# Weight sums, PSUM evictions and residual sums of a hybrid layer's channel sub-layer, arranged another way

## The chip, the cores and the metric

The kernel runs on one core of a Trainium2 chip. The metric is the device time of one execution in microseconds (us); lower is better. The kernel before takes 2641.09 us (median of three runs, 2638.81 to 2647.72).

A core has a matrix engine (TensorE, PE in the profile; PEld is its weight load), a vector engine (VectorE, DVE), a scalar engine (ScalarE, ACT), a general engine (GpSimd, POOL) and SyncE (SP), which here issues transfers (DMAs). Each engine takes its instructions strictly in the order in which the built program lists them; they wait for each other by semaphores. SBUF is the on-chip memory that all engines work in, PSUM the small memory into which the matrix engine accumulates, DRAM the large memory where inputs, outputs and scratch tensors lie.

## The reference

The reference is one decoder layer on a sequence of 512 positions and 2048 features, in 32-bit floats. A mixing sub-layer (a gated linear recurrence and an RWKV-7 head group) comes first; the change touches nothing of it. The channel sub-layer and the final norm follow, cut here to what matters:

```python
h = modulate(rms_norm(x, norm_ffn_g[l]), sh_f, sc_f)
gate, up = jnp.split(h @ w_gu[l], 2, axis=-1)
x = x + g_f[:, None, :] * ((jax.nn.silu(gate) * up) @ w_down[l])
...
return rms_norm(x, final_norm_g)
```

w_gu is 2048 x 11264 and w_down 5632 x 2048. The row g_f gates the result of the second product, feature by feature, before it is added to the residual x.

## The kernel before

**Products.** Both products are done in a Strassen-Winograd form: a pair of 2 x 2 blocks is multiplied with seven block products in place of eight. A block product's weight operand is a block of weights or a sum of blocks. Called b11, b12, b21 and b22, the four blocks go in as: product 1 takes b11, product 6 takes s = b11 + b12 + b22, product 5 takes b11 + b12, product 4 takes b21 + s, product 7 takes b12 + b22, product 2 takes b21 and product 3 takes b22. Every operand is split into a high and a low part (`whi` by a cast on ACT, L105; `wlo` by a subtraction on DVE, L106), and three matmuls, high by high, low by high and high by low, give nearly full 32-bit accuracy.

**Stages and loops.** The up projection (weights `w_gu`) has 11 column blocks m of 8 k-tiles a half. The down projection (weights `w_down`) is done in three chunks of 8, 7 and 7 k-tiles a half, each with two column blocks m. One column block runs through `half` twice: the first half makes the products 1, 6, 5, 4, the second 7, 2, 3. A half has four steps k0 of two k-tiles (or one, at the end of 7). A step loads its blocks into tiles `wraw` (tag "raw", 8 buffers of 512 KB, which the staging of the left operands shares), adds, splits, and issues twelve matmuls of 128 x 512 for each product of two k-tiles. The split tiles `whi` and `wlo` have four buffers each.

**Sums of weights.** In the first half three additions on DVE make the operands (L1269, L1270 and L1276), in the second one (L1285).

**PSUM.** Products 1 and 7 use the banks of tag "mm", 6 and 2 of "gr", 5 and 3 of "ch", two banks each, one for each half t of the rows; product 4 uses "st" and "y". When the last step's matmuls of a product are issued, `finish(p, t)` takes its PSUM out and combines it with what is kept: a copy on ACT for product 1 (L1237), and additions or subtractions on DVE for the others (L1240 for product 6, L1243 for 5, L1246 for 4, L1249 and L1250 for 7, L1254 for 2, L1257 for 3). The next column block's product 1 needs the "mm" banks that L1249 and L1250 read. The results live in tiles `ev_a`, `ev_b`, `ev_v` and `ev_w`, one buffer for each t.

**Order.** A list scheduler sets the order on every engine when the program is built, from the dependencies, its own cost estimates and priorities; code inside `tc.high_priority()` goes ahead of what is not. The sums and the splits are in such blocks; `finish` is not. At run time the order is fixed.

**Results of the down projection.** `down_end` has `put(x, t, e)` for each of the 16 result tiles (four row blocks t, four column groups e) of a chunk. Chunk 0 stores them to scratch tensors `yd` in DRAM. Chunk 1 fetches `yd` back, adds it on POOL (L1091) and stores it again. Chunk 2 fetches and adds once more, fetches the gate row (`gf`, broadcast to all partitions), multiplies on DVE (L1096), fetches the residual `x1d`, adds it on DVE (L1097), and squares on ACT for the norm (L1099). Results of e = 0 and 2 go to `xd` in DRAM and come back as `xend`; those of e = 1 and 3 stay in SBUF. All these transfers are issued by SP (L1085, L1093, L1101, L1163), in one queue with the weight loads (L1211). Behind the last chunk stand the loads of the norm's weights `fg` and `xend`, the root and reciprocal of the norm (L1166 to L1168), and 16 scalings on DVE (L1172), each with its store of the output.

## Time and profile before

| what | value |
|---|---|
| median of three runs | 2641.09 us (2638.81 to 2647.72) |
| the profiled execution's own time | 2636.42 us |
| its span, first to last instruction | 2634.3 us |
| mean granted clock of TensorE | 0.949 |
| busy over the span | PE 2345.7 us, DVE 2096.4, ACT 1117.4, POOL 260.1 |
| up projection | about 1076 to 2038 us |
| down projection | about 2038 to 2574 us |
| last matmul to the end | 2574 to 2634.3 us |

The profile is of one execution. "x52" in a row is a count; a number in square brackets behind an instruction is how long its engine sat idle ahead of it and what released it. SPq is SP's issuing queue: a wait there holds every transfer that stands behind it. The granted clock is a share of full speed. The DMA share is the mean busy share of the core's 16 DMA engines.

### The profile page before, as it was taken

What the parts mean: (1) busy time and instruction counts of PE and PEld (TensorE: products, weight loads), DVE (VectorE), ACT (ScalarE), POOL (GpSimd) and SP (SyncE); (2) the same over time, 40 slices, a digit from 0 to 9 for tenths busy, and PEclk for the clock granted to TensorE, in tenths of its full rate; (3) what the DMA queues carried; (4) which work ended last, traced back from release to release, by engine and by line L of the source; (5) the groups of instructions that cost most, each with busy time, mean ns of one, the idle gap of its engine ahead of it and who ended that gap; (6) DMA issues with size and microseconds to landing.
All of it is one profiled execution on the core that took longest, in us unless ns stands there. A gap on an engine that the chain in (4) does not pass through costs nothing. (4 is left out here: it accounts for less than half of the span.)

```text
span 2634.3 us, 32326 instructions
## 1 busy us (share of the span) xinstructions
PE 2345.7 (89%) x10992; PEld 1856.6 (70%) x10992; DVE 2096.4 (80%) x3730; ACT 1117.4 (42%) x1625; POOL 260.1 (10%) x207
## 2 busy tenths in 40 slices
PE   6999999999998989779899999999999998987980
PEld 4667777777777867557778777787777776765760
DVE  7879898999887657878788777778779988788764
ACT  3356455454464333534334434444444444333331
POOL 0000111111001000130000000000003112234101
PEclk9999999999999999789999999999999999998985
DMA  8864534454524267546667656666557767676664
GB/s 310 302 210 120 158 113 144 135 153 142 155 73 137 74 210 253 184 160 213 227 225 246 188 177 197 193 200 192 182 180 236 233 226 250 205 236 237 201 222 148
DMA packets 265977, 503.47 MB, mean 191 GB/s; under 512 B 23442, under 2 KB 48402, under 8 KB 261586
## 3 DMA queue, kind: packets, MB, share of 16 engines
q1 hardware_dynamic: 265812, 501.41, 59.0%
q8 instruction: 86, 1.41, 0.2%
q14 instruction: 79, 0.65, 0.1%
HBM read 466.84 MB, written 34.10 MB: 190 GB/s over the span
## 5 line engine op out<-in xcount | busy, mean ns | idle before, releaser
L105 ACT CAST whi<-wraw 128x1024 fp32r<-128x1024 f32 (+1 forms) x707 | 625.9, 901 | 908.2 <-DVE wraw L1270 250.8
L106 DVE TENSOR_TENSOR wlo<-wraw,whi 128x1024 fp32r<-128x1024 f32 (+1 forms) x707 | 742.0, 1067 | 245.3 <-ACT whi L105 240.9
L1227 PE MATMUL ps_mm<-whi,comb 128*128 128x512 f32 x528 | 216.7, 411 | 53.7 <-DVE ev_b L1250 34.4
L1227 PE MATMUL ps_gr<-whi,comb 128*128 128x512 f32 x528 | 217.7, 412 | 36.1 <-ACT whi L105 35.3
L124 PE MATMUL ps_mm<-hhi,whi 128*128 128x512 f32 x556 | 235.7, 426 | 8.4 <-ACT hhi L255 6.7
L199 DVE SCALAR_TENSOR_TENSOR adaq<-adaq,cbq 128x512 f32<-128x512 f32 x256 | 174.4, 688 | 73.4 <-DMA adaq<-in_w_ada 59.5
L125 PE MATMUL ps_mm<-hlo,whi 128*128 128x512 f32 x556 | 225.6, 406 | 1.1 <-DVE hlo L256 1.0
L126 PE MATMUL ps_mm<-hhi,wlo 128*128 128x512 f32 x556 | 225.9, 406 | 0.0
L1229 PE MATMUL ps_gr<-wlo,comb 128*128 128x512 f32 x528 | 214.4, 408 | 9.8 <-DVE wlo L106 9.8
L1229 PE MATMUL ps_mm<-wlo,comb 128*128 128x512 f32 x528 | 214.6, 407 | 9.5 <-DVE wlo L106 9.5
L1227 PE MATMUL ps_ch<-whi,comb 128*128 128x512 f32 x528 | 210.7, 399 | 5.1 <-DVE x L996 2.5
L1228 PE MATMUL ps_gr<-whi,comb 128*128 128x512 f32 x528 | 214.3, 406 | 0.0
L1228 PE MATMUL ps_mm<-whi,comb 128*128 128x512 f32 x528 | 214.2, 406 | 0.0
L1229 PE MATMUL ps_ch<-wlo,comb 128*128 128x512 f32 x528 | 209.4, 397 | 1.9 <-DVE wlo L106 1.9
L1228 PE MATMUL ps_ch<-whi,comb 128*128 128x512 f32 x528 | 209.9, 398 | 0.0
L1227 PEld LDWEIGHTS ps_mm<-whi,comb 128*128 128x128 f32 x528 | 103.6, 196 | 83.4 <-DVE ev_b L1250 38.4
L1227 PEld LDWEIGHTS ps_gr<-whi,comb 128*128 128x128 f32 x528 | 104.2, 197 | 65.1 <-ACT whi L105 40.3
L1229 PEld LDWEIGHTS ps_gr<-wlo,comb 128*128 128x128 f32 x528 | 103.3, 196 | 39.4 <-DVE wlo L106 15.5
L124 PEld LDWEIGHTS ps_mm<-hhi,whi 128*128 128x128 f32 x556 | 106.3, 192 | 33.0 <-ACT hhi L255 9.0
L1229 PEld LDWEIGHTS ps_mm<-wlo,comb 128*128 128x128 f32 x528 | 103.5, 196 | 35.1 <-DVE wlo L106 12.9
L125 PEld LDWEIGHTS ps_mm<-hlo,whi 128*128 128x128 f32 x556 | 106.4, 191 | 25.7 <-DVE hlo L256 5.2
L1227 PEld LDWEIGHTS ps_ch<-whi,comb 128*128 128x128 f32 x528 | 101.0, 191 | 31.1 <-DVE ev_v L1257 4.2
(386 smaller groups left out, 4620.3 us busy)
## 6 DMA issues: line engine op xcount, KB each, us to landing
wraw<-in_w_gu SPq DMA_DIRECT2D x308, 512.0 KB, 4.3
wraw<-in_w_down SPq DMA_DIRECT2D x140, 512.0 KB, 4.6
adaq<-in_w_ada SPq DMA_DIRECT2D x256, 256.0 KB, 3.5
wraw<-in_w_in SPq DMA_DIRECT2D x160, 256.0 KB, 3.1
ada<-in_w_ada SPq DMA_DIRECT2D x32, 1024.0 KB, 7.3
stage<-s SPq DMA_DIRECT2D x28, 512.0 KB, 5.0
s<-flip SPq DMA_DIRECT2D x44, 256.0 KB, 3.0
wraw<-in_w_out SPq DMA_DIRECT2D x17, 512.0 KB, 6.1
```

What stands on the lines that cost most here:

```text
L105: nc.scalar.copy(out=hi, in_=src)
L106: nc.vector.tensor_tensor(out=lo, in0=src, in1=hi.bitcast(F32), op=ALU.subtract)
L124: mm(ps, lhsT=w[0], rhs=x[0], start=start, stop=False)
L125: mm(ps, lhsT=w[0], rhs=x[1], start=False, stop=False)
L126: self.pe = mm(ps, lhsT=w[1], rhs=x[0], start=False, stop=stop).ins
L199: nc.vector.scalar_tensor_tensor(out=t, in0=t, scalar=1.0, in1=cb, op0=ALU.mult, op1=ALU.mult, accum_out=part[:, m, h:h + 1])
L1227: mm(ps[p][t], lhsT=ah, rhs=hi[:, z], start=k == 0, stop=False)
L1228: mm(ps[p][t], lhsT=al, rhs=hi[:, z], start=False, stop=False)
L1229: mm(ps[p][t], lhsT=ah, rhs=lo[:, z], start=False, stop=k == n - 1)
```

## The change

Three things are changed, all of them in the channel sub-layer.

First, two of the four weight sums move from DVE to transfers. A new helper `add` issues, on POOL's queue, a transfer from DRAM that adds what it reads to what lies in the tile. In the first half b11 is loaded twice, and b12 is added to the second copy (t1 = b11 + b12); b12 itself is no longer loaded. In the second half b22 is added to the loaded b12 (t3). The sums s and b21 + s stay on DVE.

Second, `finish` is put into a high-priority block.

Third, a result of the down projection is multiplied by its gate in every chunk, on DVE, and in the first two chunks a transfer on POOL's queue adds it to the residual `x1d` in DRAM. The `yd` tensors and the additions on POOL leave. The gate rows are fetched at the start of the second half of each m. For the odd column groups the residual is loaded ahead into tiles `xin`, and `fg`, `xin` and `xend` are loaded ahead of the last second half (chunk 2, m = 1) instead of after it.

```diff
--- before.py
+++ after.py
@@ -982,7 +982,6 @@
                     t = sd[c, e, q] = self.dram.tile([P, w, S], F32, name=f"s{c}{e}{q}")
                     for z in range(w):
                         where[base + e * n + 4 * q + z] = t[:, z]
-        yd = [[self.dram.tile([P, S], F32, name=f"yd{t}{e}") for e in range(4)] for t in range(4)]
 
 
         quads = self.x1q
@@ -1080,22 +1079,20 @@
         ss = self.fq.tile([P, 4, 4], F32, tag="ss", name="ss", bufs=1)
         kept = {}
 
-        def fetch(src, tag):
-            t = fq.tile([P, S], F32, tag=tag[0], name="fetch", bufs=tag[1])
+        def fetch(src, tag, bufs):
+            t = fq.tile([P, S], F32, tag=tag, name="fetch", bufs=bufs)
             nc.sync.dma_start(out=t, in_=src)
             return t
 
         def down_end(c):
             def put(x, t, e):
-                if c:
-                    pool_tt(out=x, in0=x, in1=fetch(yd[t][e], ("ft", 2)), op=ALU.add)
+                tt(out=x, in0=x, in1=self.gate[e], op=ALU.mult)
                 if c < 2:
-                    nc.sync.dma_start(out=yd[t][e], in_=x)
+                    nc.gpsimd.dma_start(out=self.x1d[t][e], in_=x, accum_op=ALU.add)
                     return
-                g = fetch(self.gf[:, e * S:(e + 1) * S].to_broadcast([P, S]), ("ad", 2))
-                tt(out=x, in0=x, in1=g, op=ALU.mult)
-                tt(out=x, in0=x, in1=fetch(self.x1d[t][e], ("ft", 2)), op=ALU.add)
-                junk = fq.tile([P, S], F32, tag="ad", name="junk", bufs=2)
+                x1 = self.xin[t, e] if e % 2 else fetch(self.x1d[t][e], "ft", 2)
+                tt(out=x, in0=x, in1=x1, op=ALU.add)
+                junk = fq.tile([P, S], F32, tag="cb", name="junk", bufs=1)
                 nc.scalar.activation(out=junk, in_=x, func=AF.Square, accum_out=ss[:, t, e:e + 1])
                 if e % 2 == 0:
                     nc.sync.dma_start(out=self.xd[t][e // 2], in_=x)
@@ -1135,6 +1132,24 @@
                 for second in (False, True):
                     if not z and not m and second:
                         h_second()
+                    if z and second:
+                        self.gate = {e: fetch(self.gf[:, e * S:(e + 1) * S].to_broadcast([P, S]), "ad", 2)
+                                     for e in (m, m + 2)}
+                    if z == 3 and m and second:
+                        self.xin = {}
+                        fg = self.big.tile([P, 4, S], F32, tag="h", name="fg")
+                        for e in (1, 3):
+                            v = self.cp.tile([P, 4, S], F32, tag="c", name="xin")
+                            for t in (2, 3, 0, 1):
+                                nc.sync.dma_start(out=v[:, t], in_=self.x1d[t][e])
+                                self.xin[t, e] = v[:, t]
+                        nc.sync.dma_start(out=fg, in_=i["final_g"].to_broadcast([P, D]).rearrange(
+                            "p (e n) -> p e n", n=S))
+                        for e in (0, 2):
+                            v = self.cp.tile([P, 4, S], F32, tag="c", name="xend")
+                            for t in range(4):
+                                nc.sync.dma_start(out=v[:, t], in_=self.xd[t][e // 2])
+                                kept[t, e] = v[:, t]
                     steps = self.half(st, m, second)
                     for j in range(4):
                         if not z and not m and not second:
@@ -1155,13 +1170,6 @@
                     nc.sync.dma_start(out=self.gf.rearrange("o (k p) -> p (o k)", p=P), in_=self.mod[:, 80:96])
 
 
-        fg = self.big.tile([P, 4, S], F32, tag="h", name="fg")
-        nc.sync.dma_start(out=fg, in_=i["final_g"].to_broadcast([P, D]).rearrange("p (e n) -> p e n", n=S))
-        for e in (0, 2):
-            v = self.big.tile([P, 4, S], F32, tag="h", name="xend")
-            for t in range(4):
-                nc.sync.dma_start(out=v[:, t], in_=self.xd[t][e // 2])
-                kept[t, e] = v[:, t]
         r = self.small.tile([P, 4], F32, tag="rstd", name="rstd", bufs=1)
         nc.vector.tensor_reduce(out=r, in_=ss, op=ALU.add, axis=AX.X)
         nc.scalar.activation(out=r, in_=r, func=AF.Sqrt, scale=1.0 / D, bias=self.eps[:, 0:1])
@@ -1210,6 +1218,10 @@
             t = t.rearrange("p (k n) -> p k n", n=S)[:, :w]
             nc.sync.dma_start(out=t, in_=stage["src"](m, k0, w, which).rearrange("k p n -> p k n"))
             return t
+
+        def add(t, which, k0, w):
+            nc.gpsimd.dma_start(out=t, in_=stage["src"](m, k0, w, which).rearrange("k p n -> p k n"),
+                                accum_op=ALU.add)
 
         def product(p, b, k0, w):
             with tc.high_priority():
@@ -1228,7 +1240,8 @@
                     mm(ps[p][t], lhsT=al, rhs=hi[:, z], start=False, stop=False)
                     mm(ps[p][t], lhsT=ah, rhs=lo[:, z], start=False, stop=k == n - 1)
                 if k0 + w == n:
-                    finish(p, t)
+                    with tc.high_priority():
+                        finish(p, t)
 
         def finish(p, t):
             keep, q = self.keep, ps[p][t]
@@ -1263,27 +1276,26 @@
             if not second and k0 == 0:
                 flips, self.pending = self.pending, None
             if not second:
-                b11, b12, b22, b21 = (load(z, k0, w) for z in (0, 2, 3, 1))
+                b11, t1, b22, b21 = (load(z, k0, w) for z in (0, 0, 3, 1))
+                add(t1, 2, k0, w)
                 product(1, b11, k0, w)
                 with tc.high_priority():
-                    tt(out=b11, in0=b11, in1=b12, op=ALU.add)
-                    tt(out=b12, in0=b11, in1=b22, op=ALU.add)
-                product(6, b12, k0, w)
+                    tt(out=b22, in0=t1, in1=b22, op=ALU.add)
+                product(6, b22, k0, w)
                 if flips:
                     flips(0)
                     flips(1)
                 with tc.high_priority():
-                    tt(out=b21, in0=b21, in1=b12, op=ALU.add)
-                product(5, b11, k0, w)
+                    tt(out=b21, in0=b21, in1=b22, op=ALU.add)
+                product(5, t1, k0, w)
                 if flips:
                     flips(2)
                     flips(3)
                 product(4, b21, k0, w)
             else:
-                b12, b22, b21 = (load(z, k0, w) for z in (2, 3, 1))
-                with tc.high_priority():
-                    tt(out=b12, in0=b12, in1=b22, op=ALU.add)
-                product(7, b12, k0, w)
+                t3, b22, b21 = (load(z, k0, w) for z in (2, 3, 1))
+                add(t3, 3, k0, w)
+                product(7, t3, k0, w)
                 product(2, b21, k0, w)
                 product(3, b22, k0, w)
             yield
```

The priorities move instructions. The first place is DVE where one column block of the up projection ends and the next begins (`wraw` are weights, `wlo` split parts; the number is the buffer's). Before:

```order
L106 TENSOR_TENSOR wlo_15519<-wraw_15510,whi_15518 128x1024
L1249 TENSOR_TENSOR ev_w_15241<-ps_mm_15265,ev_w_15241 128x512
L1269 TENSOR_TENSOR wraw_15510<-wraw_15510,wraw_15512 128x1024
L1250 TENSOR_TENSOR ev_b_15451<-ev_v_15221,ps_mm_15265 128x512
L1270 TENSOR_TENSOR wraw_15512<-wraw_15510,wraw_15514 128x1024
L1064 TENSOR_TENSOR ev_w_15241<-ev_w_15241,ev_b_15451 128x512
L1276 TENSOR_TENSOR wraw_15516<-wraw_15516,wraw_15512 128x1024
L106 TENSOR_TENSOR wlo_15539<-wraw_15512,whi_15538 128x1024
L106 TENSOR_TENSOR wlo_15574<-wraw_15510,whi_15573 128x1024
L106 TENSOR_TENSOR wlo_15608<-wraw_15516,whi_15607 128x1024
L1249 TENSOR_TENSOR ev_w_15249<-ps_mm_15266,ev_w_15249 128x512
L1250 TENSOR_TENSOR ev_b_15462<-ev_v_15229,ps_mm_15266 128x512
```

Here `finish` of t = 0 (L1249, L1250) stands between the sums of the next block's first step, its t = 1 stands behind three splits. With the change, at such a place:

```order
L106 TENSOR_TENSOR wlo_14844<-wraw_14794,whi_14843 128x1024
L106 TENSOR_TENSOR wlo_14878<-wraw_14868,whi_14877 128x1024
L1283 TENSOR_TENSOR wraw_14992<-wraw_14990,wraw_14992 128x1024
L1262 TENSOR_TENSOR ev_w_14599<-ps_mm_14623,ev_w_14599 128x512
L1262 TENSOR_TENSOR ev_w_14607<-ps_mm_14624,ev_w_14607 128x512
L1289 TENSOR_TENSOR wraw_14994<-wraw_14994,wraw_14992 128x1024
L1267 TENSOR_TENSOR ev_a_14537<-ps_gr_14641,ev_a_14537 128x512
L1267 TENSOR_TENSOR ev_a_14545<-ps_gr_14642,ev_a_14545 128x512
L106 TENSOR_TENSOR wlo_14897<-wraw_14872,whi_14896 128x1024
L1263 TENSOR_TENSOR ev_b_14809<-ev_v_14579,ps_mm_14623 128x512
L1263 TENSOR_TENSOR ev_b_14820<-ev_v_14587,ps_mm_14624 128x512
L1270 TENSOR_TENSOR ev_v_14579<-ps_ch_14659,ev_v_14579 128x512
```

Both rows of L1262, the first reading of "mm", and both of L1263, which gives it free, now stand together ahead of the splits of products 5 and 4, and ahead of all of them stands L1283 on wraw_14992. That is the sum s of the next block's second step, which reads wraw_14990, the tile into which the plain load and the accumulating transfer of that step went. Behind it stand L1289 (b21 + s) and L1267 (product 2 out of PSUM). The same order stands at the middle of each of the three chunks of the down projection (m = 0 to m = 1).

The second place is SP's queue in the last chunk. Before, in its last column block (`wraw` are weight loads):

```order
L1085 DMA fetch_20379<-gf_17416 128x512
L1085 DMA fetch_20408<-yd00_10428 128x512
L1211 DMA wraw_20699<-in_w_down 128x512
L1211 DMA wraw_20760<-in_w_down 128x2x512
L1085 DMA fetch_20414<-x1d00_9427 128x512
L1211 DMA wraw_20762<-in_w_down 128x2x512
L1211 DMA wraw_20764<-in_w_down 128x2x512
L1101 DMA xd31_10452<-ev_b_20361 128x512
L1085 DMA fetch_20411<-gf_17416 128x512
L1085 DMA fetch_20420<-yd02_10430 128x512
L1211 DMA wraw_20821<-in_w_down 128x2x512
L1211 DMA wraw_20823<-in_w_down 128x2x512
```

and with the change, at the start of the last second half:

```order
L1219 DMA wraw_20736<-in_w_down 128x2x512
L1098 DMA xd11_10432<-ev_v_20114 128x512
L1151 DMA xend_20724<-xd00_10429 128x512
L1151 DMA xend_20724<-xd10_10431 128x512
L1151 DMA xend_20724<-xd20_10433 128x512
L1151 DMA xend_20724<-xd30_10435 128x512
L1151 DMA xend_20729<-xd01_10430 128x512
L1151 DMA xend_20729<-xd11_10432 128x512
L1151 DMA xend_20729<-xd21_10434 128x512
L1151 DMA xend_20729<-xd31_10436 128x512
L1219 DMA wraw_20738<-in_w_down 128x2x512
L1219 DMA wraw_20795<-in_w_down 128x2x512
```

The fetches of `yd` are gone from between the weight loads, and the eight `xend` loads stand there, behind one load of weights (wraw_20736) and ahead of the next (wraw_20738).

## Prediction

> **What bounds the kernel now.** First the windows by stage (columns: window, length, busy time and count of PE, PEld, DVE, ACT and POOL, granted clock, DMA share, GB/s), since a share over the whole span mixes stages:
>
> ```profile
> 1180.00:2000.00 820.00, 784.39 (x3413) 633.06 (x3411) 643.41 (x701) 339.48 (x376) 8.31 (x3) 0.98 0.64 204
> 2000.00:2574.00 574.00, 505.72 (x2032) 393.88 (x2030) 462.59 (x433) 220.59 (x254) 124.20 (x52) 0.93 0.68 224
> 2574.00:2634.30 60.30, 0.01 (x1) 0.00 (x0) 27.62 (x39) 7.37 (x18) 9.68 (x7) 0.52 0.47 160
> ```
>
> Matmuls of one product start 0.227 us apart in the timeline below (1625.48 to 1625.71, for one), so 3413 of them need 775 us of the first window's 820 and 2032 need 461 of the second's 574. The matrix engine sets the pace; 45 us are lost in the up projection, 113 in the down projection, and all 60.3 behind the last matmul. DVE, at 643 of 820 us, is not the bound, so DVE work removed is worth only what the lost time gives back. Then the waits of PE, first of the up projection's window (1180 to 2000), then of the down projection's (2038 to 2574):
>
> ```profile
> PE ps_mm L1227 <- DVE ev_b L1250: 31.5, 11, 5.8
> ```
>
> ```profile
> PE ps_gr L1227 <- ACT whi L105: 15.8, 7, 8.6
> PE ps_gr L1229 <- DVE wlo L106: 9.8, 9, 2.5
> PE ps_mm L1229 <- DVE wlo L106: 8.7, 5, 4.2
> PE ps_mm L1227 <- ACT whi L105: 7.5, 3, 4.0
> PE ps_st L1227 <- ACT whi L105: 6.8, 2, 5.0
> PE ps_mm L1227 <- ACT ev_a L1237: 6.1, 1, 6.1
> PE ps_mm L1227 <- DVE ev_b L1250: 2.9, 2, 2.1
> ```
>
> The up projection loses its time where a column block ends: product 1 of the next waits until L1250 has freed its bank. The timeline of PE and DVE at one such place, and of PE at one of the worst:
>
> ```profile
> 1625.48 0.39 PE L1228 MATMUL ps_mm<-whi,comb 128*128 128x512 f32 x1
> 1625.71 0.39 PE L1229 MATMUL ps_mm<-wlo,comb 128*128 128x512 f32 x1
> ...
> 1626.39 0.39 PE L1229 MATMUL ps_mm<-wlo,comb 128*128 128x512 f32 x1
> 1629.14 0.50 PE L1227 MATMUL ps_mm<-whi,comb 128*128 128x512 f32 x1 [2.36 <-DVE ev_b L1250]
> ```
>
> ```profile
> 1618.05 1.23 DVE L106 TENSOR_TENSOR wlo<-wraw,whi 128x1024 fp32r<-128x1024 f32 x1 [1.53 <-ACT whi L105]
> ...
> 1628.40 0.68 DVE L1250 TENSOR_TENSOR ev_b<-ev_v,ps_mm 128x512 f32<-128x512 f32 x1
> 1629.00 0.68 DVE L1254 TENSOR_TENSOR ev_a<-ps_gr,ev_a 128x512 f32<-128x512 f32 x1
> ```
>
> ```profile
> 1372.74 0.79 PE L1227 MATMUL ps_mm<-whi,comb 128*128 128x512 f32 x1 [5.73 <-DVE ev_b L1250]
> 1373.34 0.63 PE L1228 MATMUL ps_mm<-whi,comb 128*128 128x512 f32 x1
> ...
> 1378.46 0.46 PE L1228 MATMUL ps_gr<-whi,comb 128*128 128x512 f32 x1
> ```
>
> **The tail: -34.5 us.** Behind the last matmul the results pass one by one through a chain: fetch of `yd`, POOL addition, fetch of the gate, multiplication, fetch of the residual, addition.
>
> ```profile
> 2573.62 0.40 PE L1229 MATMUL ps_ch<-wlo,comb 128*128 128x512 f32 x1
> ...
> 2616.22 0.69 DVE L1096 TENSOR_TENSOR ev_v<-ev_v,fetch 128x512 f32<-128x512 f32 x1 [3.23 <-DMA fetch<-gf]
> 2616.95 0.69 DVE L1097 TENSOR_TENSOR ev_v<-ev_v,fetch 128x512 f32<-128x512 f32 x1
> ```
>
> From 2574.0 to 2617.6 are 43.6 us. With the change gates and odd residuals lie in SBUF, and on DVE stand one eviction and thirteen multiplications and additions, which start 0.65 us apart when nothing holds them up (0.60 between the two rows at 1628 above, 0.73 from L1096 to L1097 at the end): 14 x 0.65 = 9.1. The norm, the 16 scalings and the stores stay. Gain 34.5; if the last accumulations into the residual were late it would be less, but the m = 1 results of chunk 1 are summed a whole chunk ahead.
>
> **The column ends of the up projection: +29 us.** The cast and the DVE sums, by the groups of instructions:
>
> ```profile
> L105 ACT CAST whi<-wraw 128x1024 fp32r<-128x1024 f32 (+1 forms) x707 | 625.9, 901 | 908.2 <-DVE wraw L1270 250.8 <-PE ps_mm L125 114.2 <-PE ps_ch L1228 97.2
> ...
> L1269 DVE TENSOR_TENSOR wraw<-wraw 128x1024 f32<-128x1024 f32 x68 | 87.5, 1286 | 0.6
> L1270 DVE TENSOR_TENSOR wraw<-wraw 128x1024 f32<-128x1024 f32 x68 | 86.0, 1264 | 4.6 <-DMA wraw<-in_w_down 3.7
> L1285 DVE TENSOR_TENSOR wraw<-wraw 128x1024 f32<-128x1024 f32 x68 | 84.5, 1243 | 29.0 <-DMA wraw<-in_w_gu 18.8 <-DMA wraw<-in_w_down 9.3 <-DVE wlo L106 0.5
> ```
>
> L1269 and L1285 leave, 172 us, mostly off PE's path. What counts is the row L1283 for the next block's second step, which the new order puts ahead of both L1262. It can run only when a plain load and then an accumulating transfer have landed. Call the two together X. I follow the chain backwards from the end of the block's last product (time 0; a product is 12 x 0.227 = 2.72 us). Only four split buffers exist, so product 3 of the third step, six products from the end, is split when the product four ahead of it is through, at -10 x 2.72 = -27.2, and its cast (0.9 over all forms, 1.0 taken for a full tile) and subtraction (1.2, the row at 1618) end at -25.0. That frees the raw buffer for t1 of the next block's first step. Then follow X, L1283 (1.25, as L1270), a split (1.2), L1289 (1.25) and product 7's split (1.2), 4.9 together, which frees the buffer for t1 of the second step; then X again, L1283 (1.25), two L1262 (1.3), L1289 (1.25), two L1267 (1.3), product 6's split (1.2) and L1263 (0.65), 6.95 together. PE starts at -25.0 + 2X + 11.85, a stall of 2X - 13.15.
>
> X is shown by no row: no transfer in the trace accumulates, and none of these is issued by POOL. Landing times of plain loads, from the weight loads' line and from the list of transfers:
>
> ```profile
> DMA to landing us min/median/max: 2.5/4.3/14.7
> ```
>
> ```profile
> wraw<-in_w_down SPq DMA_DIRECT2D x28, 256.0 KB, 3.6
> ...
> ada<-in_w_ada SPq DMA_DIRECT2D x32, 1024.0 KB, 7.3
> ```
>
> For the plain load I take 3.7, between the fastest and the median, since at a column end the loads go singly. For the accumulation, the lower end is the fastest plain one, 2.5; the upper is two median loads, 8.6. From 256 KB to 1024 KB a landing grows by 3.7 us, 1.2 for every 256 KB, so twice the bytes make 4.3 + 2.5 = 6.8. I take 4.8, nearer to the plain median, since read and sum may overlap: X = 8.5, bounds 6.2 and 12.3. The stall is then 3.85 us.
>
> A stall of that length has a second price. Behind 5.73 us of idleness 13 matmuls took 5.72 us from 1372.74 to 1378.46 in place of 2.95: 2.8 us more at half pace. Behind 2.36 us, at 1629, the pace was whole. At 2372.35, behind 4.03 us, it was half again:
>
> ```profile
> 2372.35 0.79 PE L1227 MATMUL ps_mm<-whi,comb 128*128 128x512 f32 x1 [4.03 <-ACT whi L105]
> 2372.94 0.63 PE L1228 MATMUL ps_mm<-whi,comb 128*128 128x512 f32 x1
> ```
>
> So I charge 2.8 with any stall nearer to four than to two. The Trainium skill ("TensorE: Matmul & The Clock Gate", section "HAM oscillation — how this bites in real kernels") puts the rule as no idle gaps beyond about 3.4 us; the trace agrees, whole after 2.36 and half after 4.03. By that rule the kernel before stood just on the safe side, and the change crosses it.
>
> Ten column ends: 10 x (3.85 + 2.8) = 66.5; off come the 31.5 of before and 2 x 2.8 for its two long ones. Net +29.4.
>
> **The down projection: -17 us.** SP's queue there stands behind the handling of `yd`; PE's waits next to it:
>
> ```profile
> 2410.90 0.32 SPq L1093 DMA_DIRECT2D yd<-ev_a  x1
> 2412.83 0.32 SPq L1093 DMA_DIRECT2D yd<-ev_v  x1
> 2413.26 5.96 SPq L1211 DMA_DIRECT2D wraw<-in_w_down  x7
> ```
>
> ```profile
> 2420.05 0.80 PE L1227 MATMUL ps_gr<-whi,comb 128*128 128x512 f32 x1 [8.62 <-ACT whi L105]
> 2482.06 0.79 PE L1227 MATMUL ps_st<-whi,comb 128*128 128x512 f32 x1 [5.03 <-ACT whi L105]
> 2534.38 0.80 PE L1229 MATMUL ps_mm<-wlo,comb 128*128 128x512 f32 x1 [4.23 <-DVE wlo L106]
> 2546.63 0.79 PE L1227 MATMUL ps_mm<-whi,comb 128*128 128x512 f32 x1 [6.12 <-ACT ev_a L1237]
> ```
>
> These four, 24.0 us, and 4 x 2.8 of clock leave: -35.2. Of the waits on `wlo`, 18.5 less the 4.23 counted, about half goes with a lighter DVE: -8. (32 more multiplications, 22 us, come on DVE; 23 steps without two sums, 58 us, cover them. Without that cover they would cost those 8.) On the other side the chunks' three middles get the new order: 3 x 6.65 - 2.9 = +17. The `xend` loads, 8 x 256 KB, stand ahead of a weight load that PE needs at once: at the rate of the second window (224 GB/s) they take 9 us, of which I let a third hide, +6. POOL's queue has the residual's accumulations, waiting for DVE, ahead of weight accumulations: 0 to 10, taken 3. Sum -35.2 - 8 + 17.1 + 6 + 3 = -17.
>
> The second half's t3 and the inner steps cost nothing: their loads go out several products of 2.72 us ahead, more than X. If X passed 12, that cover would go too.
>
> **Sum.** -34.5 + 29.4 - 17.1 = -22: span 2612 us, execution 2614 (2.1 more than the span, as before), and since the median stands 4.7 above the profiled execution, 2619 us. By X: every microsecond is worth 2 x 13 = 26 us, and nothing is won or lost at X = 9.4.
>
> **Rivals.**
> *Cheap accumulations.* X at most 7.7: the stalls are no longer than now, no clock is lost, and 13 x (2X - 13.15) replaces 13 x (2X - 10.35); the rest of the sum is -108.7. At X = 7.4 the change is 21.5 - 108.7 = -87, 2554 us. For it speaks the fastest load, 2.5; against it the median, 4.3, without any sum. The Trainium skill ("DMA: Bandwidth & Descriptors", section "Anatomy of one DMA — SWDGE (gpsimd) path") fits POOL-issued transfers by 2.0 us plus bytes at 436 GB/s, for 512 KB an estimate of 3.2 us. By that figure X would be 6.9 and this rival would hold; no run here shows it.
> *Dear accumulations: slower.* One mechanism: DVE stands at L1283 of the second step, with the PSUM evictions behind it. From X = 9.7 on the kernel is slower; at X = 11 the sum is +43, 2684 us. For it: 6.8 for twice the bytes, so X = 10.5; against: nothing else need change.
> *Saturated transfers: slower.* A first-half and second-half step go from 7 transfers to 9. At 0.64 busy, 9/7 makes 0.82; if an accumulation counts twice, 11/7 makes 1.0, and if three times, 13/7 makes 1.19 and PE would follow the transfers, about +150 us. Against it: 9/7, the plain count, leaves a fifth of the engines' time.
> *The gain of the tail or of SP's queue is not there*, because a residual arrives late: -22 + 35 = +13, counted under the dear case.
>
> **How the numbers follow.** Forecast (X 7.8 to 9.4) 0.40, cheap 0.29, dear 0.25, saturated 0.06. About 0.3%, 8 us, is what a measurement of this kernel can tell from no change; that is X between 9.05 and 9.7. Of the forecast's 0.40, 0.30 is faster and 0.10 within; all of cheap is faster; of dear 0.02 is within and 0.23 slower. Faster 0.59, same 0.12, slower 0.29. The likeliest case alone spans 2580 to 2642; the range, with X from about 7 to 11, is 2545 to 2685.
>
> **What would show it.** Right: L1283 on DVE at column ends waiting for an accumulated `wraw`, PE waiting on `ev_b` at about 4 us, granted clock about 0.5 behind it; no `yd` on SP, 25 to 27 us from last matmul to end. Wrong: accumulations landing well away from 4.8 us; column ends without a stall; PE waits inside the column blocks, which would say that transfers are the bound.

## The result, and the profile after

The changed kernel takes 2873.09 us (median of three runs) against 2639.95 us for the kernel before beside it (median of four). A fourth run of the changed kernel, at a granted clock of 0.65, took 3291.97 us and is left out here and in all differences below. The ratio is 1.0892, 95% interval 1.0844 to 1.094: slower by 9%, where 2619 us and a range of 2545 to 2685 us were predicted. The profiled execution took 2871.0 us, with a span of 2869.2 us.

By stage in the profiled executions (the stages are bounded by the issue of the first weight load of the up projection, that of the down projection, the end of the last matmul, and the end):

| | up projection | down projection | behind the last matmul |
|---|---|---|---|
| before | 962.2 us | 535.6 | 60.3 |
| predicted move | +29.4 | -17.1 | -34.5 |
| changed | 1131.4 | 625.6 | 32.1 |
| move | +169 | +90 | -28 |

The windows of the changed kernel by stage (columns as in the prediction) show PE short of work in both projections and the granted clock down to 0.91 and 0.89. DVE is busy for 674 us of 1131, a smaller share than before (643 of 820), so it is idle, not overloaded:

```profile
1080.00:2211.00 1131.00, 932.79 (x3829) 733.27 (x3829) 674.30 (x722) 410.12 (x459) 155.62 (x109) 0.91 0.76 212
2211.00:2837.00 626.00, 489.50 (x1901) 379.72 (x1899) 372.74 (x391) 204.01 (x237) 140.97 (x104) 0.89 0.82 222
2837.00:2869.20 32.20, 0.12 (x1) 0.00 (x0) 22.23 (x37) 7.36 (x18) 0.00 (x0) 0.54 0.34 130
```

What the transfers take, which no row of before showed, stands on the page of the changed kernel (queues, and issues with their median from issue to landing):

```profile
q1 hardware_dynamic: 256020, 483.58, 51.4%
q0 software_dynamic: 40576, 77.61, 16.4%
...
wraw<-in_w_gu SPq DMA_DIRECT2D x308, 512.0 KB, 5.2
wraw<-in_w_down SPq DMA_DIRECT2D x140, 512.0 KB, 6.0
...
wraw<-in_w_gu POOLq DMA_DIRECT2D x88, 512.0 KB, 7.6
...
wraw<-in_w_down POOLq DMA_DIRECT2D x40, 512.0 KB, 7.7
```

In the median an accumulation takes 7.6 us where 4.8 was taken. A plain load of the up projection takes 5.2; those of t1 alone take 4.8, where 3.7 was taken. The waits of PE and then of DVE in the up projection (1180 to 2000 us):

```profile
PE ps_gr L1239 <- DVE ev_a L1267: 38.7, 5, 9.1
PE ps_mm L1239 <- ACT ev_a L1066: 26.5, 3, 9.9
PE ps_st L940 <- DVE ev_a L1067: 25.6, 7, 4.6
PE ps_ch L1241 <- DVE wlo L106: 19.1, 8, 6.8
```

```profile
DVE wraw L1283 <- DMA wraw<-in_w_gu: 170.6, 28, 11.7
```

The wait is where the prediction put it: DVE stands at the sum L1283 until an accumulated tile lands, and PE stands behind the evictions. One column end shows the whole course. DVE, PE and POOL there, and the record of the one plain load of t1 that went out between them:

```profile
1605.09 1.23 DVE L1283 TENSOR_TENSOR wraw<-wraw 128x1024 f32<-128x1024 f32 x1 [8.48 <-DMA wraw<-in_w_gu]
1606.23 1.22 DVE L106 TENSOR_TENSOR wlo<-wraw,whi 128x1024 fp32r<-128x1024 f32 x1
1607.37 1.22 DVE L1289 TENSOR_TENSOR wraw<-wraw 128x1024 f32<-128x1024 f32 x1
1608.50 4.62 DVE L106 TENSOR_TENSOR wlo<-wraw,whi 128x1024 fp32r<-128x1024 f32 x4
1621.96 1.22 DVE L1283 TENSOR_TENSOR wraw<-wraw 128x1024 f32<-128x1024 f32 x1 [8.84 <-DMA wraw<-in_w_gu]
1623.11 1.28 DVE L1262 TENSOR_TENSOR ev_w<-ps_mm,ev_w 128x512 f32<-128x512 f32 x2
...
1625.43 1.28 DVE L1267 TENSOR_TENSOR ev_a<-ps_gr,ev_a 128x512 f32<-128x512 f32 x2
1626.63 1.22 DVE L106 TENSOR_TENSOR wlo<-wraw,whi 128x1024 fp32r<-128x1024 f32 x1
...
1640.32 1.23 DVE L1283 TENSOR_TENSOR wraw<-wraw 128x1024 f32<-128x1024 f32 x1 [3.39 <-DMA wraw<-in_w_gu]
```

```profile
1617.94 0.39 PE L1241 MATMUL ps_ch<-wlo,comb 128*128 128x512 f32 x1
1626.27 0.77 PE L1239 MATMUL ps_gr<-whi,comb 128*128 128x512 f32 x1 [7.94 <-DVE ev_a L1267]
...
1628.92 0.63 PE L1239 MATMUL ps_mm<-whi,comb 128*128 128x512 f32 x1
1629.35 0.63 PE L1240 MATMUL ps_mm<-whi,comb 128*128 128x512 f32 x1
```

```profile
1614.64 1.20 POOL L1223 DMA_DIRECT2D wraw<-in_w_gu  x1 [16.64 <-DMA wraw<-in_w_gu]
```

```profile
L1219 SPq DMA_DIRECT2D wraw<-in_w_gu x1: 368/368/368, 1609.7 to 1609.7; - x1
...
DMA to landing us min/median/max: 4.3/4.3/4.3
```

The sum of the first step runs at 1605.09. The split behind it ends at 1609.6 and frees a raw tile; the load of t1 for the second step goes out at 1609.7 and lands 4.3 us later, at 1614.0. POOL issues the accumulation at 1614.64, and the sum of the second step runs at 1621.96. So X, load and accumulation together, was 12.3 us here. The first sum's own X, from a load issued at 1591.2, was 13.9. Over all 44 t1 of the up projection X was 13.2 in the median, 10.9 to 19.7 (from the issue of the plain load to the landing of the accumulation, matched in order of issue). Then the split at 1626.63 frees the tile for the third step, whose sum runs at 1640.32. It is a round: sum, split, load, accumulation, next sum. From sum to sum it took 16.9 and 18.4 us; a step's four products need 4 x 2.72 = 10.9 on PE.

Behind the last matmul the chain of fetches is gone, as predicted. DVE's last two additions start at 2846.91, and the norm's reduction then waits for the squares on ACT:

```profile
2846.91 1.28 DVE L1094 TENSOR_TENSOR ev_b<-ev_b,xin 128x512 f32<-128x512 f32 x2
...
2852.80 0.63 ACT L1096 ACTIVATE junk<-ev_v 128x512 f32<-128x512 f32 x1
...
2853.56 0.17 DVE L1174 TENSOR_REDUCE rstd<-ss 128x4 f32<-128x16 f32 x1 [5.37 <-ACT junk L1096]
```

### The profile page after: what moved, and what is told of

It is laid out like the page before. It is cut to its first block, busy times and chain, and to the rows that moved or that the text cites. A ratio compares the mean times of both kernels' runs of the same rounds, so it can differ in the third digit from the quotient of the medians.

```text
span 2869.2 us, 32338 instructions
## 1 busy us (share of the span) xinstructions
PE 2399.1 (84%) x10992; PEld 1881.9 (66%) x10992; DVE 1944.7 (68%) x3626; ACT 1117.9 (39%) x1625; POOL 379.1 (13%) x343
## 3 DMA queue, kind: packets, MB, share of 16 engines
q1 hardware_dynamic: 256020, 483.58, 51.4%
q0 software_dynamic: 40576, 77.61, 16.4%
## 5 line engine op out<-in xcount | busy, mean ns | idle before, releaser
L1239 PE MATMUL ps_gr<-whi,comb 128*128 128x512 f32 x528 | 226.4, 429 | 142.4 <-DVE ev_a L1267 85.8
L1283 DVE TENSOR_TENSOR wraw<-wraw 128x1024 f32<-128x1024 f32 x68 | 82.3, 1211 | 349.5 <-DMA wraw<-in_w_gu 209.4
L1239 PE MATMUL ps_mm<-whi,comb 128*128 128x512 f32 x528 | 227.5, 431 | 73.1 <-ACT whi L105 45.4
L1241 PE MATMUL ps_mm<-wlo,comb 128*128 128x512 f32 x528 | 224.0, 425 | 20.6 <-DVE wlo L106 20.3
L1223 POOL DMA_DIRECT2D wraw<-in_w_gu x88 | 106.0, 1205 | 895.0 <-DMA wraw<-in_w_gu 637.8
L1240 PE MATMUL ps_mm<-whi,comb 128*128 128x512 f32 x528 | 223.1, 423 | 0.0
L1239 PEld LDWEIGHTS ps_gr<-whi,comb 128*128 128x128 f32 x528 | 108.7, 206 | 172.6 <-ACT whi L105 117.3
L1240 PE MATMUL ps_gr<-whi,comb 128*128 128x512 f32 x528 | 220.5, 418 | 0.0
L1239 PEld LDWEIGHTS ps_mm<-whi,comb 128*128 128x128 f32 x528 | 109.9, 208 | 102.4 <-ACT whi L105 49.1
L1241 PEld LDWEIGHTS ps_ch<-wlo,comb 128*128 128x128 f32 x528 | 100.9, 191 | 51.0 <-DVE wlo L106 28.9
```

The lines of the kernel that those rows point to most:

```text
L1223: nc.gpsimd.dma_start(out=t, in_=stage["src"](m, k0, w, which).rearrange("k p n -> p k n"), accum_op=ALU.add)
L1239: mm(ps[p][t], lhsT=ah, rhs=hi[:, z], start=k == 0, stop=False)
L1240: mm(ps[p][t], lhsT=al, rhs=hi[:, z], start=False, stop=False)
L1241: mm(ps[p][t], lhsT=ah, rhs=lo[:, z], start=False, stop=k == n - 1)
L1283: tt(out=b22, in0=t1, in1=b22, op=ALU.add)
```

## The experiments

Ratios are to the kernel before in the same series, with a 95% interval. "Changed" is the changed kernel.

### Which part costs: all weight sums back on DVE

```diff
-                b11, t1, b22, b21 = (load(z, k0, w) for z in (0, 0, 3, 1))
-                add(t1, 2, k0, w)
+                b11, b12, b22, b21 = (load(z, k0, w) for z in (0, 2, 3, 1))
...
+                    tt(out=b11, in0=b11, in1=b12, op=ALU.add)
+                    tt(out=b12, in0=b11, in1=b22, op=ALU.add)
...
-                add(t3, 3, k0, w)
+                    tt(out=b12, in0=b12, in1=b22, op=ALU.add)
```

> The changed kernel with all four weight sums back on DVE and plain loads; the early evictions and the residual's accumulation stay. Theory A (the loss is the weight accumulations: 5.2 us for the plain load and 7.6 for the accumulating one in the trace of the change, in series, with DVE's PSUM evictions queued behind the sum that waits): the loss goes and the tail's and SP queue's gains stay, 2640 - 29 - 35 = 2575 us, 2550 to 2600. Theory B (the new priority of the evictions holds the splits up): still slower than before, 2700 or more. Theory C (the residual's accumulation in DRAM and the 32 gate multiplications): the down projection stays near 625 us, 2640 or more in all.

Measured: 2579.28 us, ratio 0.9792 (0.9774 to 0.981). Theory A's 2575 is met, and B and C fall. Its windows by stage:

```profile
1075.00:2012.00 937.00, 886.06 (x3821) 708.70 (x3821) 761.28 (x809) 408.68 (x460) 64.22 (x21) 0.97 0.65 206
2012.00:2538.00 526.00, 466.56 (x1908) 366.84 (x1906) 427.66 (x441) 201.82 (x237) 98.95 (x55) 0.95 0.73 221
```

Up projection 937 us, down projection 526. So the weight accumulations alone cost the changed kernel 294 us, 194 of them in the up and 100 in the down projection. The other two parts are worth 55 us to the kernel before.

### t3 or t1

> The changed kernel with the first half's sums back on DVE; only the second half's t3 is accumulated by a transfer. Theory A as on record in the prediction (t3 goes out well ahead, no DVE instruction waits for it between evictions): within 15 us of the run with all sums on DVE, about 2575 to 2590. Theory D (any accumulating transfer costs PE about the same, through the raw buffers that it holds for some 13 us or through the transfer engines): about half of the loss comes back, 2680 to 2760.

> The changed kernel with the second half's t3 summed on DVE again; only t1 is accumulated by a transfer. Theory A: nearly the whole loss is still there, 2820 to 2880, column ends of the up projection 95 to 98 us apart. Theory D: 2700 to 2780, column ends about 89 us apart.

t3 alone: 2622.18 us, 0.9959 (0.9942 to 0.9976). t1 alone: 2830.55 us, 1.0749 (1.0715 to 1.0783). t1 carries 251 of the 294 us, as theory A had it, and theory D fails in both runs. But t3 is not free: 43 us over the run with all sums on DVE, where at most 15 were expected. By stage its cost is 12 us in the up and 26 in the down projection. Between 1200 and 2000 us it costs nothing: 3417 matmuls in either run. It gains nothing there either, though t3's sums have left DVE. In the down projection PE waits longer for `whi`; its waits there, first with t3 accumulated, then with all sums on DVE:

```profile
PE ps_mm L1239 <- ACT whi L105: 39.7, 8, 7.4
PE ps_gr L1239 <- ACT whi L105: 22.8, 8, 7.0
```

```profile
PE ps_gr L1239 <- ACT whi L105: 18.6, 8, 7.6
PE ps_mm L1239 <- ACT whi L105: 17.7, 5, 7.4
```

62.5 us against 36.3 are the 26 us. What made the casts late there was not taken apart; the share of the transfer engines rises there from 0.73 to 0.81.

### t1 by transfers only in the last two steps of a half

```diff
-            if not second:
+            if not second and k0 < 4:
+                b11, b12, b22, b21 = (load(z, k0, w) for z in (0, 2, 3, 1))
...
+            elif not second:
                 b11, t1, b22, b21 = (load(z, k0, w) for z in (0, 0, 3, 1))
                 add(t1, 2, k0, w)
```

> The changed kernel with DVE sums in the first two steps of a first half, t1 accumulated by transfers only in its last two steps, so that no sum that waits for an accumulation stands among the evictions at a column end; t3 accumulated as in the change. Theory A: column ends lose their stall, blocks 83 to 87 us apart, 2580 to 2640. Theory D: half of t1's transfers remain, and with them the loss in proportion: 2700 to 2780, blocks above 90 us.

Measured: 2743.92 us, 1.042 (1.0399 to 1.0441). Theory A, as first stated, fails here, and theory D's range is met: the evictions at the column end wait for no accumulation, and half of t1's cost is still there (2743.9 - 2622.2 = 122 of 251). PE's wait (1180 to 2000 us) has moved into the block, to product 6 of the second step:

```profile
PE ps_gr L1241 <- DVE wlo L106: 47.7, 10, 6.0
```

Ten times 4.8 us. The second step's own sums are on DVE and in time. But their split stands in DVE's order behind the sum of the third step (L1300), which waits for an accumulation. DVE and PE at one of these places:

```profile
1599.14 1.23 DVE L1300 TENSOR_TENSOR wraw<-wraw 128x1024 f32<-128x1024 f32 x1 [3.91 <-DMA wraw<-in_w_gu]
...
1602.55 3.49 DVE L106 TENSOR_TENSOR wlo<-wraw,whi 128x1024 fp32r<-128x1024 f32 x3
```

```profile
1603.82 0.80 PE L1241 MATMUL ps_gr<-wlo,comb 128*128 128x512 f32 x1 [5.80 <-DVE wlo L106]
```

So it is not the column end alone that costs: inside the block too, a sum that waits for its accumulation makes late what DVE has behind it.

### What of X costs: the same transfers without the adding

These two kernels leave the sums t1 and t3 out: the second transfer overwrites the tile.

```diff
             nc.gpsimd.dma_start(out=t, in_=stage["src"](m, k0, w, which).rearrange("k p n -> p k n"),
-                                accum_op=ALU.add)
+                                )
```

> The changed kernel with the 136 weight transfers on POOL's queue as plain ones: they overwrite the tile in place of adding to it, so that the two sums are left out and the output is not the reference's. The plain load and the second transfer stay in series. Theory A (the length of the series, X, sets the loss, 26 us for each microsecond of it; X was 5.2 + 7.6 = 12.8): if a plain one from POOL lands after 6 us, X is 11 and the time about 2830 us. Theory E (the adding in the transfer engines is what costs, by their load): the landing falls to about 5 us and the time to 2700 or less.

and with `nc.sync` in place of `nc.gpsimd`:

> The same, with the second transfer issued plain on SP's queue: again the sums are left out and the tile is only overwritten. Theory A: two plain landings in series, X about 4.8 + 4.8 = 9.6, by 26 us for each microsecond below 12.8 about 2795 us, though SP's queue now waits between the two and holds later loads behind, which can make it worse. Theory E: no adding, so near the kernel with the sums on DVE, 2580 to 2640.

From POOL: 2734.0 us, 1.036 (1.0304 to 1.0415). From SP: 2589.57 us, 0.9812 (0.9754 to 0.9871). POOL's queue and its transfers' landing in the first, and the list of SP's issues (both transfers of t1 among them) in the second:

```profile
q0 software_dynamic: 23680, 77.61, 9.6%
...
wraw<-in_w_gu POOLq DMA_DIRECT2D x88, 512.0 KB, 5.6
```

```profile
wraw<-in_w_gu SPq DMA_DIRECT2D x396, 512.0 KB, 4.9
```

Both undercut both expectations of theory A (2830 and 2795), while the second transfer and its wait are still there: SP waited 61 times for the first landing (1180 to 2000 us):

```profile
SPq L1223 <- DMA wraw<-in_w_gu: 95.7, 61, 6.4
```

So the loss is not in proportion to X from zero on; below a certain length it nearly vanishes. Over the t1 of the up projection, X was 9.6 us in the median with SP, 11.2 with POOL and 13.2 in the change; the kernels took 10, 155 and 294 us more than the one with all sums on DVE. Between them that is 70 to 90 us for each microsecond of X, where theory A had 26. What POOL's queue carries changes along with X, so X is not the only difference between the three. Theory E's range is met with SP, and fails with POOL: without adding, its transfers still cost those 155 us.

### Parts two and three apart

> The kernel before with only the evictions put into the high-priority block. The kernel with all parts but the weight accumulations had its up projection 25 us shorter than before. Theory A (column ends: the 31.5 us of waits for ev_b leave with the priority): 2634 - 25 = 2610 us. Rival F (those 25 us come from the other part, or the priority delays the down projection): 2625 to 2650.

> The kernel before with only the third part: gates in every chunk, the residual accumulated in DRAM, residuals and xend loaded ahead; evictions and weight sums as before. Theory A: the tail is 27 to 28 us shorter, the down projection 10 us, the up projection as before: about 2597 us. Rival F: with late evictions the multiplications that follow them are late too, and the down projection gives the gain back: 2610 to 2630.

Only the early evictions: 2613.65 us, 0.9907 (0.9872 to 0.9943), close to theory A. Only the third part: 2576.7 us, 0.9769 (0.9731 to 0.9806), 20 us better than expected; its down projection took 510.6 us (535.6 before) and its tail 28.9. Together they gave 2579, no better than the third alone: of the 24 us that the evictions win in the up projection (937.3 for 961.6), 19 are lost in the down projection (525.8 for 510.6) and in the tail (33.0 for 28.9).

### DVE's place, or the raw tiles

```diff
-                with tc.high_priority():
+                if k0 == 2:
                     tt(out=b22, in0=t1, in1=b22, op=ALU.add)
+                else:
+                    with tc.high_priority():
+                        tt(out=b22, in0=t1, in1=b22, op=ALU.add)
```

> The changed kernel with the sum s of the second step (k0 = 2) alone outside the high-priority block, so that at a column end all evictions of PSUM stand ahead of it on DVE. Theory O (what costs is DVE's place: evictions queued behind a sum that waits): the column-end stall goes in most of the 17 blocks, 17 x 8 to 12 us, 2690 to 2750 us. Theory B (what costs is that t1's tile cannot be filled in time: with eight raw tiles its load goes out when the step two before is split, and plain load and accumulation then take 13 us): the wait only moves to product 6 of the second step, 2830 to 2880.

```diff
-        self.open_weights(ctx, "wf", 1024, 8, 4)
+        self.open_weights(ctx, "wf", 1024, 10, 3)
```

> The changed kernel with ten raw weight tiles in place of eight, and three split buffers in place of four to make room. Theory B: t1's load goes out two tiles, about two products or 5.4 us, earlier in every step; 70 to 150 us of the loss come back, 2730 to 2810. Theory O, or any theory in which the transfers' number or the order of DVE sets the loss: 2850 or more, since fewer split buffers can only cost.

> The same buffers with the weight sums on DVE (against the kernel with all sums on DVE, 2579 us): what ten raw tiles and three split buffers are worth by themselves. Both theories: within 15 us of 2579, 2565 to 2595; a larger move has to be taken off the reading of the run beside it.

Evictions ahead of the sum: 2808.34 us, 1.066 (1.0607 to 1.0712), 65 us less than the change and between the two theories. PE's column-end wait is now at the transposes that follow, nine of them, behind the late sum:

```profile
PE ps_st L940 <- DVE ev_w L1063: 81.7, 9, 16.8
```

Ten raw tiles: 2885.66 us, 1.0953 (1.0897 to 1.1009). With the sums on DVE the same buffers gave 2569.17 us, 0.9752 (0.9706 to 0.9797). So with early evictions and DVE sums the buffers are harmless, and they bring nothing to the change: theory B, as stated, fails. That the three split buffers took back what the ten raw tiles gave is not excluded. The order of DVE at the column end fits this. In the change the last split of the block (wlo_14844) stands ahead of the second step's sum (wraw_14992); with ten tiles the sum stands ahead of it, so the tile that this split frees comes free later:

```
L1283 TENSOR_TENSOR wraw_14992<-wraw_14990,wraw_14992 128x1024
L1289 TENSOR_TENSOR wraw_14994<-wraw_14994,wraw_14992 128x1024
L1262 TENSOR_TENSOR ev_w_14599<-ps_mm_14623,ev_w_14599 128x512
L106 TENSOR_TENSOR wlo_14844<-wraw_14794,whi_14843 128x1024
```

That this order is the whole reason was not tried.

### The accumulations alone on the kernel before

> The kernel before with the two weight accumulations alone: no priority for evictions, results of the down projection as before. Theory A (the accumulations are the loss): the parts add up as 2634 + (2879 - 2579) = 2934 us, 2900 to 2960. Rival G (the accumulations cost much only where the evictions stand early): 2650 to 2800.

Measured: 2903.4 us, 1.102 (1.0967 to 1.1074). The accumulations cost 269 us without the other parts and 294 with them: early evictions are not their condition, and rival G fails.

### Breaking the round

```diff
+        ahead = None
...
-                b11, t1, b22, b21 = (load(z, k0, w) for z in (0, 0, 3, 1))
-                add(t1, 2, k0, w)
+                if k0 == 0:
+                    ahead = load(0, k0, w)
+                    add(ahead, 2, k0, w)
+                t1 = ahead
+                b11 = load(0, k0, w)
+                if k0 + w < n:
+                    w2 = min(2, n - k0 - w)
+                    ahead = load(0, k0 + w, w2)
+                    add(ahead, 2, k0 + w, w2)
+                b22, b21 = (load(z, k0, w) for z in (3, 1))
```

> The changed kernel with the plain load and the accumulation of t1 for the next step requested at the start of this one; the same transfers, sums, buffers and priorities. Loop theory: in the change each t1 load waits for a raw tile that a split frees which stands on DVE behind the sum s of the step before, so sum, split, load, accumulation and next sum run round, 13.4 + 3.5 us a step where PE needs 4 x 2.72 = 10.9, three times in each block, some 18 us of it. Here the load waits for a split ahead of that sum, two steps share one round, and the loss goes but for t3's share: up projection 945 to 985 us in place of 1131, 2610 to 2700 us in all. Rival H (it is the number and length of accumulating transfers, or DVE's place, and not the round): above 2780.

And t1 merely loaded ahead of b11 in its own step:

> The changed kernel with t1 loaded first in its own step in place of second: the load goes out one tile earlier, but the split that frees its tile still stands behind the sum of the step before on DVE. Loop theory: the round stays, at most one split (1.2 to 2.7 us) shorter a step: 2780 to 2860. A theory by which any earlier load brings back its lead (2.7 us a step, 68 steps): below 2720.

One step ahead: 2713.01 us, 1.0294 (1.0254 to 1.0333); t1 first: 2853.23 us, 1.0822 (1.079 to 1.0855). With the same number of transfers, sums and buffers, 160 us come back when the load no longer waits for a split behind the last sum, and 20 when it goes out one tile earlier but still waits for such a split. X itself did not shrink: 13.7 us in the median one step ahead, against 13.2 in the change. One more thing moved in that kernel: on DVE one of the two L1262 and one of the two L1263 now stand ahead of the second step's sum. That this alone gave the 160 us is unlikely: all the evictions ahead of that sum gave 65. DVE's wait for the accumulated tiles halves (1180 to 2000 us; 170.6 in the change):

```profile
DVE wraw L1292 <- DMA wraw<-in_w_gu: 82.8, 32, 9.8
```

The starts of the sum s on DVE show the pace of the first half in every kernel. Medians over five to seven blocks of the up projection from 1420 us on, in us from one sum to the next, and from the fourth to the first of the next block:

| kernel | 1 to 2 | 2 to 3 | 3 to 4 | to the next block | block |
|---|---|---|---|---|---|
| before | 13.7 | 14.3 | 10.6 | 44.1 | 82.7 |
| sums on DVE | 12.1 | 9.8 | 13.0 | 45.3 | 80.3 |
| second transfer plain, SP | 12.6 | 17.0 | 12.8 | 39.6 | 82.0 |
| second transfer plain, POOL | 16.4 | 17.2 | 9.8 | 47.6 | 91.0 |
| changed | 16.8 | 18.7 | 11.2 | 51.4 | 98.2 |
| ten raw tiles | 16.7 | 15.8 | 16.8 | 51.4 | 100.7 |
| t1 first | 15.6 | 16.0 | 12.2 | 52.0 | 95.8 |
| t1 one step ahead | 10.5 | 14.9 | 8.2 | 50.9 | 84.5 |

In the change the first two intervals are the round's 17 to 19 us; one step ahead the three make 33.6 us in place of 46.7, less than with the sums on DVE (34.9). A long interval alone is no loss: the second transfer from SP has one of 17.0, and a block no longer than before.

Where PE loses the time is seen in the starts of its matmuls: all that lies between two starts beyond 0.227 us is lost (the transposes between them count as lost in every kernel). Medians over the six or seven whole blocks of the up projection that begin between 1420 and 1960 us, in us:

| kernel | first 36 matmuls (products 1, 6, 5 of the first step) | next 60 (the second step) | other 240 |
|---|---|---|---|
| before | 2.9 | 2.0 | 0.6 |
| sums on DVE | 0.2 | 2.9 | 0.7 |
| changed | 11.4 | 8.2 | 1.7 |
| t1 by transfers only in the last two steps | 0.2 | 12.5 | 0.7 |
| evictions ahead of the sum | 10.2 | 2.2 | 1.6 |
| t1 one step ahead | 4.5 | 2.1 | 0.7 |

One step ahead, the second step's loss is gone and the column end's is more than halved. What stays there, 4.5 us where the sums on DVE have 0.2, no run took apart. The kernel's total missed the expected 2610 to 2700 by 13 us, its up projection (1018 us) the 945 to 985 by 33.

> The kernel before with the third part alone (2577 us) and ten raw weight tiles with three split buffers, which gave 10 us to the kernel with all sums on DVE: if that gain is the buffers' own, 2560 to 2575; if it was tied to the early evictions, 2575 to 2600.

Measured: 2618.52 us, 0.9934 (0.9912 to 0.9955), 42 us worse than the third part with eight tiles. What the buffers gave was tied to early evictions; with late ones they cost. The best of all kernels here are the third part with ten tiles, early evictions and sums on DVE (2569 us) and the third part alone (2577 us); they were run in different series, and their intervals overlap.

## Why the prediction was wrong

**What bounds the kernel** held: PE sets the pace, and DVE work removed is worth nothing by itself. 172 us of DVE sums left, and DVE only stood idle longer.

**The tail, -34.5**: the mechanism was right, -28 was measured. Forgotten were the squares on ACT, which come one behind the other at the end: 5.4 us of waiting at the reduction, where the kernel before had 0.85. And DVE had eighteen instructions there and not fourteen: 11.1 us, where 9.1 were summed.

**The column ends, +29, measured +169 for the up projection.** The first step that failed is the size of X. It was taken as 3.7 + 4.8 = 8.5. It was 12.3 and 13.9 in the timeline, 13.1 in the mean of these two, beyond the upper bound of 12.3. In the prediction's own formula the stall is then 2 x 13.1 - 13.15 = 13.1. The chain itself was right to within 2 or 3 us: in the timeline product 1 starts at 1628.92, 10.8 us behind the last matmul of the block before (1617.94, and 0.23 for itself). PE stood at "gr" and not at "mm" because part of product 6 stands ahead of product 1 on PE in the changed program; the prediction did not look at that order.

But the column ends are only half of what the up projection lost. The block grew by 15.5 us (82.7 to 98.2). By the table of PE's losses 8.5 of it came at the column end, where the formula with 2.8 for the clock, less 3.7 a block of before, gives 12.2. Another 6.2 came in the second step, for which the prediction had nothing.

The charge for the clock was about right where it was taken: behind 7.94 us of idleness PE ran at half pace (starts 0.43 us apart). But the border that the prediction drew between two and four microseconds is not what the trace of before shows. There PE ran at half pace also behind gaps about as short as the 2.36 us that left it whole, one of them shorter:

```profile
1457.44 0.79 PE L1227 MATMUL ps_mm<-whi,comb 128*128 128x512 f32 x1 [2.44 <-DVE ev_b L1250]
...
2300.23 0.80 PE L1227 MATMUL ps_mm<-whi,comb 128*128 128x512 f32 x1 [2.15 <-DVE ev_b L1250]
```

So the length of the gap alone does not decide it.

The dear rival was the right one, at a chance of 0.25, and its point of decision was too late: by the sum's formula X = 13.1 gives 13 x (26.2 - 10.35) - 108.7 = +97, and +235 was measured between the profiled executions. Most of the rest lies in the next step.

**"The second half's t3 and the inner steps cost nothing ... If X passed 12, that cover would go too."** This is the second step that failed. X did pass 12, and the consequence was not put into the sum. In the first half the second and third sums are 18.7 us apart, against 9.8 with the sums on DVE. In the down projection t1 alone costs 75 us over the sums on DVE (600.8 against 525.8), 12.5 for each of its six column blocks, and not only for the three middles that the new order of evictions touches. The formula's two X belong to a round which the prediction wrote down for one place only. The kernel with t1 one step ahead shows it: with the same transfers, the same X and the same sums, 160 us came back.

**The down projection, -17, measured +90.** Without weight accumulations it was -10 with early evictions and -25 without. In those kernels the sums are still on DVE, so of the terms for `yd`, lighter DVE and `xend` only -35 + 6 = -29 applies, and by the prediction's own words up to 8 for the uncovered multiplications comes on. So the gain on SP's queue was real and of about the right size. The early evictions, a cost that no term held without accumulations, take about 15 us of it. t1's 75 and t3's 26 make the rest: -25 + 15 + 75 + 26 = +91.

**The cheap rival** had for it an estimate of 3.2 us for a transfer of 512 KB issued by POOL, from a fit in the Trainium skill ("DMA: Bandwidth & Descriptors", section "Anatomy of one DMA — SWDGE (gpsimd) path"). Under the load of this kernel the plain ones of that size took 5.6 us in the median, 4.0 at the least, and the accumulating ones 7.6; the measurement decides, and the rival falls. **Saturation** falls too for the up projection: with t3 alone the transfer engines were as busy as in the change (0.78 and 0.77 between 1200 and 2000 us), and nothing was lost there. For t3's 26 us in the down projection it is not excluded.

## What to carry to other kernels

A transfer that takes work from an engine with slack gives nothing and adds its latency wherever that work stands in a chain; ask first whether the chain closes on itself through buffers and an in-order engine. Where it does, the pace is the round's length, not the sum of busy times. Here neither more buffers (nothing) nor a better place for one waiting instruction (65 us) helped as much as requesting the transfer one turn earlier (160 us). Price an operation that no row shows at the far bound too, and put that bound through every step of the kernel, not through the one place where it was first seen.

## What the runs showed of the hardware

An accumulating transfer of 512 KB cost the transfer engines twice what a plain one from the same queue cost, though its bytes are counted once. From the q0 rows, with the residual's accumulations (8.39 MB, 2.2% of 2571 us in the run with sums on DVE, 57 us) taken off: 16.4% of 2869 is 471, less 57 is 414 us for 69.2 MB of adding; 9.6% of 2733 is 262, less 57 is 205 us for the same 69.2 MB plain. It also held POOL longer: 1.20 us an issue against 0.72 for a plain one, in the median of each run. And with the adding gone, a transfer of up-projection weights issued by POOL still landed later than one issued by SP in the same place, 5.6 us against 4.9 in the median.
